# Two-layer inference step on one core: everything behind the mixing in two token halves, with the pages' attention interleaved with the mixing and the first half

## The chip, the cores and the metric

The kernel runs on one core of a Trainium2 chip. The metric is the device time of one execution in microseconds (us); less is better. A core has a matrix engine (TensorE, in the profile PE, with its weight loads as PEld), a vector engine (VectorE, DVE), a scalar engine (ScalarE, ACT), a general engine (GpSimd, POOL), and SyncE (SP), which here issues most of the transfers. Each engine works through its own list of instructions in order and waits at semaphores for the others.

## The reference

One step of a hybrid decoder with two layers, D = 1024, for a prompt of 1024 tokens and for 8 samples with 4 new tokens each, which share all weights. Per layer, each part ahead of its residual add begins with an RMS norm:

```python
z = rms_norm(x, norm_mix) @ w_in                 # one projection for all heads
o_gdn, s_new = gated_delta_rule(...)             # 4 DeltaNet heads, causal short convolution before
keys = concatenate([past_k, kd]); vals = concatenate([past_v, vd])   # samples: 4096 past tokens in pages
o_diff = diff_attention(qd, keys, vals, ...)     # 4 differential attention heads
x = x + concatenate([o_gdn, o_diff]) @ w_out
qc = rms_norm((rms_norm(x, norm_cross) @ w_cq).reshape(B, L, 4, 128), qnorm_cross)
x = x + memory_attention(qc, mem_k, mem_v).reshape(B, L, 512) @ w_co     # 256 memory tokens
hf = rms_norm(x, norm_ffn)
gt, ffn_new = causal_dwconv(hf @ w_gate, ffn_buf, conv_ffn)              # width 3 along the tokens
x = x + (silu(gt) * (hf @ w_up)) @ w_down                                # 2816 wide
```

Of the parts behind `o_diff`, only the convolution in the MLP links tokens with each other: a token needs the gate rows of the two tokens before it. The next layer's mixing needs all tokens.

## The kernel before

The residual stream is kept with features on the partitions: 8 tiles of 128 features by 1056 columns, the 1024 prompt tokens and then the 32 sample tokens. A product of two float32 operands is made of three matmuls: each operand is split into a rounded part and a rest (ScalarE casts, VectorE or GpSimd subtracts), and `mm3` (L346 to L348) adds high by high, low by high and high by low. Weights come from DRAM in units of 512 KB: a load by SyncE into one of two `raw` buffers (L322), a cast on ScalarE (L325, tile `whi`) and a subtraction on GpSimd (L326, tile `wlo`), into four buffers of each (`Weights(..., 2, 4)`).

A layer has two stages. In the **mixing**, the projections, DeltaNet (`gdn`, tiles with psG) and the prompt's attention (`attn`) are Python generators that `interleave` runs side by side by their costs; beside all of them run the pages (`dec`, then `dec_end`): page loads by SyncE (`kn`, `vn`), a transpose on VectorE (L639), scores (L643) and values (L667) on TensorE. Such an interleaving only sets the order in which instructions are handed to a scheduler; the scheduler then writes each engine's list by priorities and by a simulated time line (`prio` shifts the priority). The mixing leaves its outputs in DRAM, `ogs` and `oas`, by tiles of tokens; only the last attention head goes through SBUF (`lasts`).

**Behind the mixing**, everything runs once over all 1056 columns in three chunks of CH = 352 (`csl`): the output projection (`linear_add`, its last two feature tiles chunk by chunk, and a norm as soon as a chunk is complete), the cross-attention (projection of the queries; `cross_prompt` by token tiles of 128, interleaved with `cross_samples`), `w_co`, the next norm, and the MLP in pairs of feature tiles (FG = 2): per tile the gate and the up products, the convolution and the multiplication, and then per pair the down products, added to `x` (L1986). In `norm_chunk` ScalarE squares, VectorE adds, TensorE sums over the features with a matrix of ones, ScalarE makes the inverse root, and VectorE and GpSimd scale and split. After the last pair the first layer's chunks are normed for the next layer and written to DRAM (`xsc`); after the second layer the tiles are transposed and written out.

PSUM banks for the stream are taken in turn (`psA`, four); behind the mixing a fifth (`psB`) joins them (`turn[0] = 1`).

## Time and profile before

| | |
|---|---|
| Three runs | 4203.21, 4212.04 and 4216.07 us; median 4212.04 |
| The profiled execution | 4210.3 us from its first to its last instruction; its time outside that span isn't listed |
| Mean granted TensorE clock | 0.948 |
| TensorE, weight loads | 3816.0 us (91%), 3397.5 us (81%) |
| VectorE, ScalarE, GpSimd | 2314.2 us (55%), 1259.7 us (30%), 1150.3 us (27%) |
| DMA | 581.55 MB, 138 GB/s over the span |

Read along time, the first layer's mixing lasts until about 1104 us, its pages from 190 to 1050; its output projection starts at 1110.58, and its MLP lasts until about 2139. The second layer's mixing follows, and what is behind that ends at 4210.3. A share of the span is an average over these stages; what a stage is bound by is seen in a window of it. An engine that is idle costs nothing unless another engine waits for it, and the waits of TensorE show where that is so.

### The profile page before, as it was taken

To read this page: it belongs to the slowest core of one execution; us is meant where nothing else is said; L and a number is where in the kernel's file an instruction comes from. 1 tells how busy PE (TensorE), PEld (TensorE's weight loads), DVE (VectorE), ACT (ScalarE), POOL (GpSimd) and SP (SyncE) were. 2 spreads that over 40 slices of the span, in tenths; PEclk is the share of its full clock that TensorE was granted. 3 is DMA by queue.
4 is the path that set the end of the run, shared out by engine and by line. 5 is a ranking of instruction groups with operands and counts; after the bars stand their busy time and mean duration, and the time that the engine had idled before them with its cause. 6 is when DMAs were issued, how large, how long until landed. Compare 5 with 4: busy or idle time off the path is not lost. (4 is left out here: it accounts for less than half of the span.)

```text
span 4210.3 us, 74231 instructions
## 1 busy us (share of the span) xinstructions
PE 3816.0 (91%) x27524; PEld 3397.5 (81%) x27524; DVE 2314.2 (55%) x4305; ACT 1259.7 (30%) x2773; POOL 1150.3 (27%) x1130
## 2 busy tenths in 40 slices
PE   6988888888899999999988889877879999999999
PEld 5877765565798999999977777745669889999999
DVE  7554655666445644444477456556753564545454
ACT  4322423333334312121233134332342531212121
POOL 6641321311331322222235223122123132222221
PEclk8999998898899999999999999988989999999999
DMA  5698889998412111111139988899732211111111
GB/s 176 195 277 224 226 222 230 234 234 218 142 46 81 46 46 46 46 46 46 49 114 282 267 229 221 237 247 241 202 103 87 87 40 46 46 46 46 46 46 57
DMA packets 549602, 581.55 MB, mean 138 GB/s; under 512 B 67053, under 2 KB 376248, under 8 KB 549240
## 3 DMA queue, kind: packets, MB, share of 16 engines
q1 hardware_dynamic: 503765, 546.67, 47.4%
q10 hardware_dynamic: 43811, 25.81, 2.1%
q8 instruction: 217, 3.56, 0.4%
q0 software_dynamic: 1664, 4.33, 0.3%
q14 instruction: 145, 1.19, 0.1%
HBM read 498.45 MB, written 78.20 MB: 137 GB/s over the span
## 5 line engine op out<-in xcount | busy, mean ns | idle before, releaser
L346 PE MATMUL psA<-hh,whi 128*128 128x352 f32 x3072 | 1012.6, 330 | 27.1 <-ACT whi L325 23.0
L347 PE MATMUL psA<-hl,whi 128*128 128x352 f32 x3072 | 1004.7, 327 | 0.8 <-POOL hl L384 0.8
L348 PE MATMUL psA<-hh,wlo 128*128 128x352 f32 x3072 | 1001.8, 327 | 0.0
L326 POOL TENSOR_TENSOR wlo<-raw,whi 128x1024 fp32r<-128x1024 f32 (+1 forms) x308 | 529.6, 1727 | 1361.6 <-ACT whi L325 1353.2
L346 PEld LDWEIGHTS psA<-hh,whi 128*128 128x128 f32 x3072 | 587.2, 191 | 39.6 <-ACT whi L325 28.2
L347 PEld LDWEIGHTS psA<-hl,whi 128*128 128x128 f32 x3072 | 588.8, 192 | 10.8 <-issue 8.3
L348 PEld LDWEIGHTS psA<-hh,wlo 128*128 128x128 f32 x3072 | 585.9, 191 | 12.6 <-issue 11.2
L325 ACT CAST whi<-raw 128x1024 fp32r<-128x1024 f32 (+1 forms) x308 | 236.8, 781 | 898.6 <-issue 436.7
L639 DVE STREAM_TRANSPOSE T<-kn 128x1024 f32<-128x1024 f32 x256 | 315.9, 1237 | 197.5 <-DMA kn<-in_cache_k_dram 195.0
L346 PE MATMUL psA<-hi,hh 128*128 128x256 f32 (+3 forms) x864 | 253.2, 294 | 48.4 <-DVE cxn L730 44.6
L1986 DVE TENSOR_TENSOR x<-x,psA 128x352 f32<-128x352 f32 x422 | 214.3, 520 | 134.4 <-PE psA L348 130.4
L346 PE MATMUL psA<-ah,whi 128*128 128x352 f32 x844 | 275.4, 326 | 0.0
L347 PE MATMUL psA<-al,whi 128*128 128x352 f32 x844 | 271.2, 321 | 0.0
L348 PE MATMUL psA<-ah,wlo 128*128 128x352 f32 x844 | 266.2, 325 | 0.0
L348 PE MATMUL psA<-hi,hl 128*128 128x256 f32 (+3 forms) x864 | 249.3, 290 | 3.9 <-POOL hl L384 3.3
L347 PE MATMUL psA<-lo,hh 128*128 128x256 f32 (+3 forms) x864 | 250.2, 290 | 0.0
L667 PE MATMUL psC<-vn,pT 128*32 128x512 f32 x1024 | 148.7, 674 | 103.7 <-DMA vn<-in_cache_v_dram 86.0
L346 PEld LDWEIGHTS psA<-hi,hh 128*128 128x128 f32 (+1 forms) x864 | 160.0, 186 | 60.4 <-issue 42.2
L643 PE MATMUL psB<-T,lq 128*32 128x128 f32 x4096 | 147.3, 289 | 63.8 <-DVE T L639 41.1
L347 PE MATMUL psB<-hl,whi 128*128 128x352 f32 x576 | 188.1, 327 | 10.3 <-DVE hl L384 7.1
L346 PE MATMUL psB<-hh,whi 128*128 128x352 f32 x576 | 188.7, 328 | 6.9 <-ACT hh L381 6.9
L1956 DVE COPY fraws<-psA 128x32 f32<-128x32 f32 x36 | 6.9, 191 | 341.0 <-ACT fraw L1955 341.0
(528 smaller groups left out, 7317.1 us busy)
## 6 DMA issues: line engine op xcount, KB each, us to landing
kn<-in_cache_k_dram SPq DMA_DIRECT2D x512, 256.0 KB
vn<-in_cache_v_dram SPq DMA_DIRECT2D x512, 256.0 KB
raw<-in_w_gate_dram SPq DMA_DIRECT2D x44, 512.0 KB
raw<-in_w_up_dram SPq DMA_DIRECT2D x44, 512.0 KB
raw<-in_w_down_dram SPq DMA_DIRECT2D x44, 512.0 KB
qksc<-ctt ACTq DMA_DIRECT2D x128, 128.0 KB
raw<-in_w_in_dram SPq DMA_DIRECT2D x128, 128.0 KB
gdsc<-cdst SPq DMA_DIRECT2D x24, 528.0 KB
```

The costliest lines, as they stand in the source:

```text
L325: s_.copy(hi, raw)
L326: g_.tensor_tensor(lo, raw, hi.bitcast(F32), op=ALU.subtract)
L346: t_.matmul(ps, ahi, bhi, start=(i == 0), stop=False)
L347: t_.matmul(ps, ahi, blo, start=False, stop=False)
L348: t_.matmul(ps, alo, bhi, start=False, stop=(i == n - 1))
L639: v_.transpose(T[:, 2 * hf:2 * hf + 2].rearrange("p s j b -> p (s j b)"), kn.rearrange("p s d -> p (s d)"))
L643: t_.matmul(sc[32 * c:32 * c + 32, (S % 4) * P:(S % 4 + 1) * P], lq[:, 4 * c + j, :], T[:, :, 4 * c + j, :], start=(j == 0), stop=(j == 3))
L667: t_.matmul(po[32 * i:32 * i + 32, :], pT[:, i, S, :], vn[:, i, :], start=(S == 0), stop=(S == 7))
L1956: v_.tensor_copy(raws[:, :, 2:6], ps[:, NP - 2 * CH:CH].rearrange("p (b t) -> p b t", t=4))
L1986: v_.tensor_tensor(x[:, ot, cs], x[:, ot, cs], ps[:, 0:CH], op=ALU.add)
```

## The change

The generator `post(lo, n, smp)` does all that stood behind the mixing, for `n` prompt tokens from `lo` on and, if `smp`, for the sample tokens too. It is run with tokens 0 to 511, in two chunks of 256 (in the MLP one of 512, except for its first feature tile and its last down products), and then with tokens 512 to 1023 and the samples, in two chunks of 272. Each half loads and splits its weights. The first is chained behind the mixing in the stream that is interleaved with the pages, and the two streams' totals are changed from 527 against 128 to 950 against 152. The two last gate columns of the first half go to the second in `carry`. In the first layer the residual stream of each half goes to `xsc`; the norms for the next layer are made in the second half, those of tokens 0 to 511 from columns that are read back (`early`, at two places of its MLP), those of the rest behind its last down products. In the second layer each half writes its output. The last attention head's output goes through DRAM like the others'. `norm_chunk` takes any columns, and its sum and its root share a buffer name. The fifth PSUM bank joins in the second half only. Comments are gone, which shifts lines: L346 before is L347 after.

```diff
+POST = 500.0
...
+    def __init__(self, pool, name, n=NT):
+        self.pool, self.name, self.n = pool, name, n
+        self.t = [pool.tile([P, KT // 2, n], F32R, tag=f"{name}{i}", name=f"{name}{i}") for i in range(2)]
...
-    def norm_chunk(c, x, gain, hh, hl, wk, light=False, nb=1, late=0):
-        """RMS norm of a chunk, in two parts. light: little work for the vector engine."""
-        cs = csl(c)
-        acc = None if light else wk.tile([P, CH], F32, name="nacc", tag="nacc", bufs=nb)
+    def norm_chunk(cs, xk, gain, hh, hl, wk, light=False, nb=1, late=0):
+
+
+        w = cs.stop - cs.start
+        acc = None if light else wk.tile([P, w], F32, name="nacc", tag="nR", bufs=nb)
         ps = psG()
         for kk in range(4):
-            sq = wk.tile([P, 2, CH], F32, name="nsq", tag="nsq", bufs=2 * nb)
-            s_.activation(sq, x[:, 2 * kk:2 * kk + 2, cs], AF.Square)
+            sq = wk.tile([P, 2, w], F32, name="nsq", tag="nsq" if light else "nhf", bufs=4 if light else 3)
...
+        R = wk.tile([P, w], F32, name="nR", tag="nR", bufs=nb)
...
+    carry = cp.tile([P, FT, 2], F32, name="carry")
...
-                if h < 3:
-                    QX(13).dma_start(oas[c][:, h, :], od)
-                else:
-                    lasts.append((c, od))
+                QX(13).dma_start(oas[c][:, h, :], od)
...
-        for _ in interleave((rest(), 80 + 172 + 45 + 230.0), (chain(ahead(dec(), TUNE[6]), ahead(dec_end(), TUNE[8])), 8 * TUNE[0] * (float(XP[16]) if l == 0 else 1))):
...
+        w_cm, nw_cm, X_cm = (pool(f"{nm}{l + 1}", side=HS) for nm in ("w", "nw", "X"))
+        W = nw = X = None
...
+        def post(lo, n, smp):
+
+
+            nonlocal W, nw, X, Hn_cm, hn, ln, prep_cm, pre_next
+            NL = n + (NS if smp else 0)
+            SUB = NL // 2
+            subs = [slice(0, SUB), slice(SUB, NL)]
+            tiles = [(lo // P + i, P) for i in range(n // P)] + ([(8, NS)] if smp else [])
+            if W is None:
+                W = Weights(w_cm.__enter__(), 2, 4)
+            with prio(UPRI):
+                us = [unit(a["w_out"][l], KT, k) for k in range(int(XP[9]))]
+            if nw is None:
+                nw = nw_cm.__enter__()
+                X = X_cm.__enter__()
+            Hp_cm = pool(f"P{l}{lo}", side=HS)
+            Hp = Hp_cm.__enter__()
+            hh = Halves(Hp, "ph", NL)
+            hl = Halves(Hp, "pl", NL)
+            for i, (t, w_) in enumerate(tiles):
+                cs = slice(i * P, i * P + w_)
+                ot_ = stp.tile([P, KT * P], F32, name="ot", tag="ot", bufs=2).rearrange("p (k t) -> p k t", t=P)
+                for hf in range(2):
+                    o_ = ot_[:, 4 * hf:4 * hf + 4, 0:w_]
+                    nc.sync.dma_start(o_, ogs[t] if hf == 0 else oas[t // 4][:, :, (t % 4) * P:(t % 4) * P + w_])
+                    split(hh.t[hf][:, :, cs], hl.t[hf][:, :, cs], o_, g_ if (hf == 0 and OSP) or OSP > 1 else v_)
+            x = X.tile([P, KT, n + NS], F32, name="x", tag="x", bufs=1)
+            for k in range(KT):
+                nc.sync.dma_start(x[:, k, 0:NL], xsc[:, k, lo:lo + NL])
+            yield 1.0
...
+            wv = int(XP[9])
+            for ot, c in wave(wv, wv, 2) + [(t, c) for t in range(wv, 6) for c in range(2)] + [(t, c) for c in range(2) for t in (6, 7)]:
+                cs = subs[c]
+                ps = lin_ps(us[ot][0], us[ot][1], hh, hl, KT, cs)
+                v_.tensor_tensor(x[:, ot, cs], x[:, ot, cs], ps, op=ALU.add)
+                if c and wv - 1 <= ot < 5:
+                    us.append(unit(a["w_out"][l], KT, ot + 1))
+                if ot == 5:
+                    us.append(unit(a["w_out"][l], KT, 6 + c))
+                yield 24 * SUB / 2200.0
+                if ot == 7:
+                    norm_chunk(cs, xat(x, cs), g_cross, hh, hl, nw)
+                    yield 0.5
...
+            ssp = psG((P, 17)) if not smp else psC((P, 17))
...
+                nt = n // P
...
+            yield from interleave((cross_prompt(), n / P * 2.7 + 7), *([(cross_samples(), 8 * 2.5 + 3)] if smp else []))
...
+            if smp and more:
+
+                Hn_cm = pool(f"H{l + 1}", side=XS)
+                Hn = Hn_cm.__enter__()
+                hn, ln = Halves(Hn, "hh"), Halves(Hn, "hl")
+                xp = [ln.t[i][:, :, 0:lo].bitcast(F32) for i in range(2)]
+                for i in range(2):
+                    nc.sync.dma_start(xp[i], xsc[:, 4 * i:4 * i + 4, 0:lo])
+
+                def early(c):
+                    cs = slice(c * 256, c * 256 + 256)
+                    norm_chunk(cs, lambda k, m: xp[k // 4][:, k % 4:k % 4 + m, cs] if m > 1 else xp[k // 4][:, k % 4, cs], pv[l + 1][:, 48:56], hn, ln, nw)
...
+            for th in range(2):
+                for c in range(2):
+                    cs = subs[c]
+                    for ot in range(4 * th, 4 * th + 4):
+                        u = wco[ot // 2]
+                        oc = slice(P * (ot % 2), P * (ot % 2) + P)
+                        ps = lin_ps(u[0][:, :, oc], u[1][:, :, oc], hh, hl, 4, cs)
+                        v_.tensor_tensor(x[:, ot, cs], x[:, ot, cs], ps, op=ALU.add)
+                        yield 12 * SUB / 2200.0
+                    if th:
+                        norm_chunk(cs, xat(x, cs), g_ffn, hh, hl, nw)
+                        yield 0.5
+                    elif c:
+                        nxt = gu(0)
+
+
+            wide = subs if smp else [slice(0, NL)]
+            f0 = 0
+            while f0 < FT:
...
+                    if lo:
+                        g_.tensor_copy(raw[:, 0:2], carry[:, f])
+                    else:
+                        g_.memset(raw[:, 0:2], 0.0)
...
+                    chs = wide if f else subs
+                    order = [(kind, cs) for cs in chs for kind in "gu"] if f == 0 else [(kind, cs) for kind in "gu" for cs in chs]
...
+                        if not smp:
+                            g_.tensor_copy(carry[:, f], raw[:, n:n + 2])
+                            return None
...
+                        if more and f in (4, 8):
+                            early(f // 4 - 1)
...
+                chs = subs if lastg else wide
+                for ot, cs in [(ot, cs) for cs in chs for ot in range(8)]:
+                    w_ = cs.stop - cs.start
+                    ps = psA()[:, 0:w_]
+                    mm3(ps, [((dn[fi][0][:, ot], dn[fi][1][:, ot]), (ah[:, fi, cs], al[:, fi, cs])) for fi in range(gs_)])
+                    v_.tensor_tensor(x[:, ot, cs], x[:, ot, cs], ps, op=ALU.add)
+                    yield 3 * gs_ * w_ / 2200.0
+                    if lastg and ot == 7 and more:
+                        if smp:
+                            norm_chunk(slice(lo + cs.start, lo + cs.stop), xat(x, cs), pv[l + 1][:, 48:56], hn, ln, nw)
+                        s_.dma_start(xsc[:, :, lo + cs.start:lo + cs.stop], x[:, :, cs])
+            ff_cm.__exit__(None, None, None)
+            if not more:
+                with pool(f"xout{lo}", side=XS) as ip:
+                    for i, (t, m) in enumerate(tiles):
...
+        HALF = NP // 2
+        for _ in interleave((chain(rest(), post(0, HALF, False)), 450.0 + POST), (chain(ahead(dec(), TUNE[6]), ahead(dec_end(), TUNE[8])), 152.0)):
             pass
-        turn[0] = 1
...
+        turn[0] = 1
+        for _ in post(HALF, HALF, True):
+            pass
...
```

The order of the instructions at three places. First TensorE, where the first layer's mixing ends. L667 before and L674 after are the pages' value products, L987 and L1198 parts of DeltaNet, L1422 and `oraw` the prompt's attention, and the products with `whi` the first of the output projection. Before:

```order
L667 MATMUL psC<-vn,pT 32x512 x4
L1422 MATMUL psA<-aV,aT 128x128 x4
...
L1422 MATMUL psA<-aV,aT 128x128 x8
L1439 MATMUL psA<-c_ident,oraw 128x128 x4
L346 MATMUL psA<-hh_16392,whi 128x352
L347 MATMUL psA<-hl_16394,whi 128x352
```

After:

```order
L674 MATMUL psC<-vn,pT 32x512 x4
L987 MATMUL psG<-X,U 128x128 x4
...
L1445 MATMUL psA<-c_ident,oraw 128x128 x4
L1080 MATMUL psG<-c_ident,oy 128x128 x4
L347 MATMUL psA<-ph_13237,whi 128x256 x3
L348 MATMUL psA<-pl_13239,whi 128x256
```

The first row of each is the pages' last value product of the layer. In the whole list it is row 3455 before and row 3442 after; the first product of the output projection is row 3547 before and row 3544 after. Its width went from 352 to 256 columns.

Then SyncE at the same place: `vn` is a page's values, `raw<-in_w_out` a unit of the output projection's weights, `ot` the operands of that projection by token tiles, from DeltaNet (`og`) and attention (`oa`), and `x<-xsc` the residual stream. Before:

```order
L608 DMA vn<-in_cache_v_dram 32x4x512
...
L1692 DMA mv<-out_p_mem_v_dram 128x2x512
L263 DMA c_sel_17313<-in_cst_dram 128x32
L1673 DMA ot<-og_78 128x512
L1673 DMA ot<-oa_85 128x3x128
L1673 DMA ot<-og_79 128x512
L1673 DMA ot<-oa_85 128x3x128
L322 DMA raw<-in_w_out_dram 128x8x128 x2
L1673 DMA ot<-og_80 128x512
```

After:

```order
L615 DMA vn<-in_cache_v_dram 32x4x512
...
L1448 DMA oa_86<-od 128x512
L323 DMA raw<-in_w_out_dram 128x8x128 x2
L1083 DMA og_83<-gate 128x512
L1660 DMA x<-xsc 128x512 x3
L323 DMA raw<-in_w_out_dram 128x8x128
L1660 DMA x<-xsc 128x512 x5
L323 DMA raw<-in_w_out_dram 128x8x128
L1683 DMA mkT<-msc 128x1024
L1656 DMA ot<-og_78 128x512
L1656 DMA ot<-oa_85 128x4x128
```

The first row is again the last page load. Four of the operand loads stood ahead of the first weights; now the weights and the residual stand ahead of the first operands, and a store of the attention's output (`oa_86<-od`) ahead of the weights.

Last TensorE in the cross-attention: `mkT,qc` are scores of the prompt (256 memory tokens), `mkn` transposes of the samples' memory keys, `cred` sums for the norm of the queries, and `phx` transposes of probabilities. Before, all tokens:

```order
L1752 MATMUL psA<-mkT,qc 128x256 x4
L1823 MATMUL psG<-c_ident,mkn 128x128 x8
L396 MATMUL psC<-cred,c_sel_17313 32x8 x4
L397 MATMUL psC<-cred,c_sel_17313 32x1
L1752 MATMUL psA<-mkT,qc 128x256 x2
L1752 MATMUL psB<-mkT,qc 128x256 x2
L1752 MATMUL psA<-mkT,qc 128x256 x2
L1823 MATMUL psG<-c_ident,mkn 128x128 x8
```

After, the first half:

```order
L1716 MATMUL psG<-cred,c_sel_14182 32x4 x4
L1749 MATMUL psA<-mkT,qc 128x256 x6
L1716 MATMUL psG<-cred,c_sel_14182 32x4 x4
L1749 MATMUL psA<-mkT,qc 128x256 x2
L1716 MATMUL psG<-cred,c_sel_14182 32x4 x4
L1749 MATMUL psA<-mkT,qc 128x256 x4
L1772 MATMUL psG<-c_ident,phx 128x128 x4
L1749 MATMUL psA<-mkT,qc 128x256 x2
L1772 MATMUL psG<-c_ident,phx 128x128 x4
L1749 MATMUL psA<-mkT,qc 128x256 x2
L1772 MATMUL psG<-c_ident,phx 128x128 x8
L1782 MATMUL psA<-plx,mv 128x256 x4
```

The samples' products that stood between the prompt's are in the second half now; the first has the prompt's alone.

## Rows read from the trace of the kernel before

**Rows 1.** Windows: busy us of each engine, with counts, clock and DMA; mixing, MLP

```profile
core 0: us, PE busy (x) PEld busy (x) DVE busy (x) ACT busy (x) POOL busy (x), PEclk, DMA share, GB/s
190.00:1050.00 860.00, 727.93 (x6243) 563.39 (x6244) 502.41 (x1023) 276.75 (x725) 210.22 (x298) 0.91 0.91 235
1500.00:2100.00 600.00, 600.00 (x3735) 592.81 (x3735) 286.90 (x465) 114.13 (x170) 136.83 (x102) 1.00 0.16 47
```

**Rows 2.** Waits of TensorE on the pages: us in total, times, longest us

```profile
PE psC L667 <- DMA vn<-in_cache_v_dram: 86.0, 49, 4.3
PE psB L643 <- DVE T L639: 41.1, 36, 5.9
```

**Rows 3.** Windows: two norms, cross-attention of both layers, change of layer, end

```profile
1200.00:1240.00 40.00, 36.00 (x218) 34.41 (x217) 34.01 (x42) 18.50 (x29) 20.50 (x11) 1.00 0.09 27
1355.00:1385.00 30.00, 22.36 (x113) 20.20 (x111) 27.49 (x35) 14.81 (x21) 16.15 (x9) 0.83 0.12 35
1255.00:1330.00 75.00, 72.02 (x586) 59.46 (x585) 39.93 (x99) 41.05 (x109) 4.50 (x5) 1.00 0.33 106
3300.00:3360.00 60.00, 55.46 (x425) 43.73 (x418) 34.51 (x87) 38.16 (x104) 3.62 (x4) 0.97 0.32 97
2139.00:2178.00 39.00, 26.92 (x163) 24.77 (x161) 35.27 (x61) 17.48 (x26) 16.03 (x18) 0.87 0.29 97
4194.00:4210.30 16.30, 9.71 (x78) 8.28 (x77) 5.18 (x8) 6.54 (x12) 0.00 (x0) 0.96 0.69 266
```

**Rows 4.** Timeline of TensorE: start us, us; products of four widths

```profile
1700.01 0.32 PE L346 MATMUL psA<-hh,whi 128*128 128x352 f32 x1
...
1704.63 0.32 PE L348 MATMUL psB<-hh,wlo 128*128 128x352 f32 x1
...
258.33 0.28 PE L346 MATMUL psA<-hi,hh 128*128 128x256 f32 x1
...
259.92 0.28 PE L348 MATMUL psA<-hi,hl 128*128 128x256 f32 x1
...
2168.45 0.29 PE L347 MATMUL psA<-lo,hh 128*128 128x264 f32 x1
...
2169.92 0.28 PE L347 MATMUL psA<-lo,hh 128*128 128x264 f32 x1
...
101.83 0.39 PE L348 MATMUL psM<-whi,mlo 128*128 128x512 f32 x1
...
105.79 0.39 PE L347 MATMUL psM<-wlo,mh 128*128 128x512 f32 x1
```

**Rows 5.** Groups of ScalarE in 1255 to 1330 us: busy, mean ns, idle before

```profile
L1763 ACT ACTIVATE hhx<-psA,cmx,rq 128x256 f32<-128x256 f32 x18 | 10.0, 594 | 0.0
L1763 ACT ACTIVATION_READ_ACCUMULATOR hhx<-psA,cmx,rq 128x1 f32 x18 | 4.2, 235 | 0.0
L1776 ACT COPY hlx<-psG 128x512 f32<-128x512 f32 x9 | 5.1, 610 | 1.4 <-PE psG L1775 1.3
```

**Rows 6.** Chain that ended last, second layer's cross-attention: start us, us

```profile
3331.47 0.86 PE psB L1752 x4
3344.02 3.45 PE psA L1785 x16
3354.47 0.44 PE psG L1775 x4
```

**Rows 7.** Page: splitting of weights, whole span: busy, mean ns, idle before

```profile
L326 POOL TENSOR_TENSOR wlo<-raw,whi 128x1024 fp32r<-128x1024 f32 (+1 forms) x308 | 529.6, 1727 | 1361.6 <-ACT whi L325 1353.2
L325 ACT CAST whi<-raw 128x1024 fp32r<-128x1024 f32 (+1 forms) x308 | 236.8, 781 | 898.6 <-issue 436.7
```

**Rows 8.** Timeline of SyncE and TensorE: first output-projection load and product

```profile
1104.17 1.06 SPq L322 DMA_DIRECT2D raw<-in_w_out_dram  x2
1110.58 0.66 PE L346 MATMUL psA<-hh,whi 128*128 128x352 f32 x1 [7.69 <-ACT whi L325]
```

More of the change, by code (lines that the diff above doesn't have):

```diff
@@ L370, in norm_chunk @@
             with prio(late):
-                t_.matmul(ps[:, 0:CH], ones, acc, start=True, stop=True)
-        R = wk.tile([P, CH], F32, name="nR", tag="nR", bufs=nb)
-        s_.activation(R, ps[:, 0:CH], AF.Ln, scale=1.0 / D, bias=epsc)
+                t_.matmul(ps[:, 0:w], ones, acc, start=True, stop=True)
+        R = wk.tile([P, w], F32, name="nR", tag="nR", bufs=nb)
+        s_.activation(R, ps[:, 0:w], AF.Ln, scale=1.0 / D, bias=epsc)
         s_.activation(R, R, AF.Exp, scale=-0.5)
@@ L1329, in build @@
         at_cm = pool(f"at{l}", side=HS)
-        lasts = []
         def attn():
```

643 lines of the change are left out of this document (291 added, 352 removed).

## The prediction

> **What bounds the kernel now.** I read the windows by stage first, then the waits, then single instructions. In the long stretch behind the mixing, TensorE is busy in all of 600 us at a granted clock of 1.00 [rows 1]: there the matmul stream is the bound, with VectorE at 287 of 600 us, ScalarE at 114 and GpSimd at 137. While the pages stream beside the mixing the DMA share is 0.91 and TensorE is busy in 728 of 860 us [rows 1]. The waits name the pages there: 86.0 us for page values and 41.1 us for a transpose of page keys [rows 2]. So this kernel has two kinds of idle time that the change could touch: some 130 us of page waits in the mixing, and short joints of 3 to 12 us behind it, where a norm, the cross-attention, the next layer or the output starts [rows 3].
>
> **The change, part by part.** All below is against the profiled execution's own 4210.3 us span; the median of the runs is 1.7 us above it.
>
> *The pages.* The words of the change let the pages run beside the first half. The order of the changed kernel does not. On TensorE the last pages' product still stands about a hundred rows ahead of the first product of the output projection, as before, and on SyncE the last page load stands ahead of the first load of that projection's weights. Engines take their instructions in this order, so all pages end inside the mixing and the page waits of [rows 2] stay. I price this part at 0; below zero only if the pages moved (a rival below), above zero not, since the order in the mixing is nearly the same.
> The rows show why nothing slides over by itself: TensorE stood 86.0 us at the page products [rows 2] although other products stood behind them. The Trainium skill (TensorE: Matmul & The Clock Gate, Part 2, step ①) says the same, that matmuls stay in program order and only weight loads are pulled ahead; by it the page waits cannot move, and the sum keeps its 0.
>
> *The products.* Behind the mixing before has 11,808 products of 352 columns; the order of the changed kernel has 1,920 of 256, 2,976 of 512 and 7,872 of 272 (both 4,156,416 columns). Start to start, from [rows 4]: 352 columns (1704.63 − 1700.01)/29 = 0.1593 us; 256 columns (259.92 − 258.33)/14 = 0.1136; 264 columns (2169.92 − 2168.45)/12 = 0.1225; 512 columns (105.79 − 101.83)/17 = 0.2329. No row has 272: scaled from 256 it is 0.1207, from 264 it is 0.1262, from 352 it is 0.1231. Before: 11,808 × 0.1593 = 1881.0 us. After: 1,920 × 0.1136 + 2,976 × 0.2329 + 7,872 × 0.1231 = 218.1 + 693.1 + 969.0 = 1880.2, so −1; with the two other prices −20 and +24. I take 352's price per column because that stretch, with weight loads for every product, is the same work.
> The Trainium skill (same page, Back-to-back issue gap) gives an isolated gap of N/2.4 + 2.5 ns, a fixed price for each product that speaks against splitting. By it before is 11,808 × 149.2 ns = 1761.4 us and after 1763.8, an estimate of +2. The trace has 159.3 ns where the formula has 149.2, so its level does not hold here, and the sum goes by the rows.
>
> *The norms.* The cross-attention's norm left TensorE 4.0 us idle in its 40 us window, the feed-forward norm 7.6 in 30 us, at a clock of 0.83; VectorE was busy in 34 of 40 and 27.5 of 30 us [rows 3], so it paces them. A chunk of 352 takes it about a third of that 34 us, 11.3 us, covered by the last two tiles of the last chunk, 2 × 24 × 0.1593 = 7.6 us: 3.7 us stays bare, near the 4.0 seen. A half-width chunk takes about 8.3 us (11.3 × 264/352) against a cover of 2 × 24 × 0.1136 = 5.5: 2.8 bare. Now the norm's sum and its root share one buffer, so the second chunk's cannot overlap the first's; I take 4.5. There are twice as many: 2 × 4.5 − 4.0 = +5 for the first kind and 2 × 7.3 − 7.6 = +7 for the second, and +3 for the lowered clock once more: +15 a layer. Ends: 0 (bare time scales with width) to 25 (nothing covers the 8.3).
>
> *Cross-attention.* Before, the samples' products and the prompt's eight tiles fill each other's gaps: 3.0 us idle of 75, 4.5 of 60 [rows 3]. The first half has four tiles and no samples. ScalarE per tile: 4 × (0.594 + 0.235) for the exponentials and their sums and 2 × 0.610 for copies [rows 5], 4.5 us; four tiles 18. TensorE per tile: four scores in 0.86 and eight transposes at four in 0.44, 0.88; the 16 value products of all four tiles 3.45 [rows 6]: 4 × 1.74 + 3.45 = 10.4. Idle 18 + 4.5, one tile's chain as lead and tail, − 10.4 = 12, and 3 for the clock behind it: +15. The second half keeps the samples, and the idle time of before with them. Ends: 0 (copies go to VectorE) to 25.
>
> *MLP of the first half.* One chunk of 512. Between the last up product of a pair and the down products that need it stand 9 products, 9 × 0.2329 = 2.1 us, for a multiplication, a cast and a subtraction of 512 columns, each near the 0.610 of a 512-column copy [rows 5] or somewhat over: 1.8 to 2.7. Eleven pairs × up to 0.6: I take +3; ends 0 to 27.
>
> *Weights twice.* Gate, up, down and the three projections are loaded and split again: 164 more units, × 1727 ns on GpSimd = 283 us and × 781 ns on ScalarE = 128 us [rows 7]. Cover: the products, with GpSimd at 137 and ScalarE at 114 of 600 us [rows 1]. Price 0; without cover see the first rival.
>
> *Joints.* Between the halves the second half's operands are split while the last down products run (96 × 0.1136 = 10.9 us): +2 a layer (0 to 15). Between the mixing and the first half SyncE now issues two more weight units and the residual ahead of the first operands, and a unit waits for a raw buffer (cast and subtraction, 0.8 + 1.7 us [rows 7]). Before, the first product came 6.4 us behind the first weight load [rows 8]; now the operands come about 11 behind it, and the load itself waits for the last attention output: +9 in the first layer, +3 in the second, where they stand ahead: +12 (0 to 25). At the change of layer 12.1 us were idle [rows 3]; the norms of tokens 0–511 are now made early, in the second half's MLP, and only the last two chunks are late, behind 117 ready products: −12 (−16 to 0). The tail had 6.6 us idle [rows 3], and half of the output leaves earlier: −2.
>
> Sum: −1 + 2 × (15 + 15 + 3 + 2) + 12 − 12 − 2 = +67. Span 4277, median 4279 us.
>
> **The rivals.**
> *Slower still:* the first half is paced by its weights. A unit now lasts 24 × 0.2329 = 5.6 us instead of 72 × 0.1593 = 11.5. From load to first use took 6.4 us [rows 8], over two raw buffers some 3.5 a unit, plus GpSimd's 1.7: it should hold, but if a unit takes 6.6 it is 1 us × 66 units × 2 = +130 on the forecast, about 4400.
> *The pages move after all:* if the chip ran the pages' loads slower than the order supposes and the products behind filled in, the waits of [rows 2], 127 us, would go: 4279 − 127 = 4150. Against it: the order of both engines.
> *Not slower:* the joints scale with their width. Two half-width joints then cost what one did: norms 0 instead of +30, cross-attention 0 instead of +30 since copies move to VectorE and the clock stays up, and products at the low price, −20, with −16 at the change of layer. It decides once the joints of a layer add less than 18 us together: 4195 to 4212. For it: the bare 2.8 us above is below the 4.0 of before. Against it: the first half has no samples to fill with, and a clock of 0.83 behind a norm [rows 3].
> That the pages do not do what the words say is part of the forecast itself.
>
> **How the numbers follow.** Forecast 0.74, slower still 0.06, pages move 0.03, not slower 0.17. Of the last 0.06 ends below 4199, 0.11 within 0.3% (12.6 us, about what can be told from no change); 0.02 of the forecast lies within it too. Faster 0.03 + 0.06 = 0.09, same 0.13, slower 0.78. Range: the forecast with the ends of its terms half used gives 4225 to 4340; with part of the fourth case 4207 to 4342.
>
> **What would show it.** In the trace after: page products that end ahead of the first output-projection product, and waits for pages of about 127 us as before (the first step); pitches of 0.114, 0.123 and 0.233 us for the three widths; 4 to 5 us idle at each of four cross norms and about 7 at each feed-forward norm; about 12 us idle in each first half's cross-attention with ScalarE busy; under 3 us idle at the change of layer. It would be wrong if page products stood beside the first half, if TensorE were idle between units in its MLP, or if the total came out under 4225.

## The result and the profile after

The changed kernel took 4403.16 us (4398.64 to 4409.45, four runs) against 4209.64 for the kernel before: 1.0457 times as long, 95% interval 1.0441 to 1.0474. The profiled execution spans 4399.9 us, 189.6 more than before. 67 were forecast; the sign was right, the size was not.

The phases of both executions in us, first layer / second layer, read off the timeline by these marks: the first output-projection load (in the second half, the last down product of the first), the first score, the last value product of the cross-attention, the first and the last down product:

| phase | before | after, both halves | more |
|---|---|---|---|
| output projection, norm, queries | 155.8 / 157.2 | 183.8 / 182.8 | 28 / 26 |
| cross-attention | 63.4 / 67.0 | 75.2 / 75.0 | 12 / 8 |
| its output, norm, first MLP tiles | 101.2 / 101.3 | 114.0 / 115.5 | 13 / 14 |
| MLP from the first to the last down product | 724.6 / 722.7 | 790.2 / 775.2 | 66 / 53 |
| mixing and change of layer | | | −7 / −17 |
| end | 15.3 | 10.3 | −5 |

The MLP holds 118 of the 190 us. In windows of the kernel after (columns as in [rows 1]) the first layer's first half has its MLP in the first row, the second half in the second:

```profile
1282.00:1649.00 367.00, 352.48 (x1540) 282.45 (x1539) 192.39 (x202) 102.11 (x131) 163.85 (x105) 0.99 0.32 96
1837.00:2261.00 424.00, 401.07 (x3032) 390.55 (x3031) 260.56 (x481) 125.65 (x194) 176.25 (x130) 0.97 0.27 81
1222.00:1282.00 60.00, 51.48 (x340) 47.76 (x339) 35.56 (x56) 22.90 (x35) 24.20 (x17) 0.89 0.20 62
1783.00:1837.00 54.00, 45.28 (x344) 43.38 (x334) 37.30 (x62) 23.79 (x38) 26.68 (x20) 0.94 0.30 98
```

Where [rows 1] shows TensorE busy in all of 600 us, it now stands 15 and 23 us idle, and GpSimd is busy in 42 to 45% of the time instead of 23%. The last two rows hold the feed-forward norms of the two halves: 8.5 and 8.7 us idle, where the one norm of before had 7.6 [rows 3].

What TensorE waited for (us in total, times, longest us), first the pages:

```profile
PE psC L674 <- DMA vn<-in_cache_v_dram: 84.3, 48, 6.2
PE psB L650 <- DVE T L646: 47.5, 34, 4.3
...
PE psA L347 <- ACT ph L383: 35.3, 11, 4.9
...
PE psA L348 <- DVE al L309: 18.5, 23, 2.4
...
PE psA L347 <- DVE fcv L1999: 12.2, 19, 3.3
...
PE psA L349 <- POOL wlo L327: 10.5, 16, 1.4
```

The two page waits are those of [rows 2] (86.0 and 41.1). `ph` is the norms' rounded part; its name before is `hh`, with 13.3 us. New are the MLP's: `al`, the rest of the down products' operand, which VectorE subtracts, and `fcv`, the multiplication that frees an accumulator. One such wait in full, GpSimd, VectorE and TensorE in the kernel after (start us, us, and in brackets the idle time before):

```profile
1321.26 2.40 POOL L327 TENSOR_TENSOR wlo<-raw,whi 128x1024 fp32r<-128x1024 f32 x1 [1.46 <-ACT whi L326]
1320.27 0.69 DVE L1999 TENSOR_TENSOR fcv<-fcv,psA 128x512 f32<-128x512 f32 x1 [0.70 <-ACT fcv L295]
1321.73 2.48 DVE L309 TENSOR_TENSOR al<-fcv,ah 128x512 fp32r<-128x512 f32 x1 [0.77 <-ACT ah L308]
1322.95 0.64 PE L347 MATMUL psA<-ah,whi 128*128 128x512 f32 x2
1324.26 0.95 PE L348 MATMUL psA<-al,whi 128*128 128x512 f32 x3 [0.68 <-DVE al L309]
```

GpSimd subtracts a unit of weights until 1323.66. VectorE's `al` begins 0.47 us behind the start of that, ends 0.55 us behind its end, and takes 2.48 us. The multiplication of the same width, which was done before GpSimd began, took 0.69. TensorE waits for `al`.

### The profile page after: what moved, and what is told of

Read it like the earlier page. It is cut to its first block, busy times and chain, and to the rows that moved or that the text cites. A ratio compares the mean times of both kernels' runs of the same rounds, so it can differ in the third digit from the quotient of the medians.

```text
span 4399.9 us, 78002 instructions
## 1 busy us (share of the span) xinstructions
PE 3886.3 (88%) x28558; PEld 3324.8 (76%) x28558; DVE 2513.4 (57%) x4572; ACT 1466.1 (33%) x3071; POOL 1571.0 (36%) x1402
## 5 line engine op out<-in xcount | busy, mean ns | idle before, releaser
L327 POOL TENSOR_TENSOR wlo<-raw,whi 128x1024 fp32r<-128x1024 f32 (+1 forms) x472 | 932.4, 1983 | 1135.5 <-ACT whi L326 1105.3
L347 PE MATMUL psA<-ph,whi 128*128 128x272 f32 (+2 forms) x2784 | 880.5, 319 | 64.2 <-ACT ph L383 35.3
L348 PE MATMUL psA<-pl,whi 128*128 128x272 f32 (+2 forms) x2784 | 879.3, 317 | 14.0 <-POOL pl L386 14.0
L349 PE MATMUL psA<-ph,wlo 128*128 128x272 f32 (+2 forms) x2784 | 877.9, 316 | 0.0
L347 PEld LDWEIGHTS psA<-ph,whi 128*128 128x128 f32 x2784 | 533.4, 193 | 100.5 <-ACT ph L383 37.6
L348 PEld LDWEIGHTS psA<-pl,whi 128*128 128x128 f32 x2784 | 535.3, 192 | 47.8 <-POOL pl L386 17.0
L349 PEld LDWEIGHTS psA<-ph,wlo 128*128 128x128 f32 x2784 | 534.1, 192 | 28.7 <-POOL wlo L327 0.2
L347 PE MATMUL psA<-ah,whi 128*128 128x272 f32 (+2 forms) x948 | 304.4, 336 | 20.1 <-DVE fcv L1999 12.2
L348 PE MATMUL psA<-al,whi 128*128 128x272 f32 (+2 forms) x948 | 304.2, 333 | 18.5 <-DVE al L309 18.5
L349 PE MATMUL psA<-ah,wlo 128*128 128x272 f32 (+2 forms) x948 | 289.5, 331 | 10.5 <-POOL wlo L327 10.5
L347 PE MATMUL psA<-hi,hh 128*128 128x256 f32 (+3 forms) x864 | 254.7, 296 | 41.4 <-DVE cxn L737 33.7
L347 PE MATMUL psA<-hh,whi 128*128 128x352 f32 x768 | 257.7, 336 | 0.0
L348 PE MATMUL psA<-hl,whi 128*128 128x352 f32 x768 | 257.5, 335 | 0.0
L349 PE MATMUL psA<-hh,wlo 128*128 128x352 f32 x768 | 255.2, 333 | 0.0
L674 PE MATMUL psC<-vn,pT 128*32 128x512 f32 x1024 | 144.5, 655 | 110.0 <-DMA vn<-in_cache_v_dram 84.3
L650 PE MATMUL psB<-T,lq 128*32 128x128 f32 x4096 | 152.2, 295 | 86.8 <-DVE T L646 47.5
```

The source lines that it names most:

```text
L327: g_.tensor_tensor(lo, raw, hi.bitcast(F32), op=ALU.subtract)
L347: t_.matmul(ps, ahi, bhi, start=(i == 0), stop=False)
L348: t_.matmul(ps, ahi, blo, start=False, stop=False)
L349: t_.matmul(ps, alo, bhi, start=False, stop=(i == n - 1))
L650: t_.matmul(sc[32 * c:32 * c + 32, (S % 4) * P:(S % 4 + 1) * P], lq[:, 4 * c + j, :], T[:, :, 4 * c + j, :], start=(j == 0), stop=(j == 3))
L674: t_.matmul(po[32 * i:32 * i + 32, :], pT[:, i, S, :], vn[:, i, :], start=(S == 0), stop=(S == 7))
```

## The experiments

Times are medians beside runs of the kernel before on the same chip (4211 to 4214 us). "Changed" is the kernel after.

**Do the pages move? `apart`.** The pages are interleaved with the mixing alone:

```diff
-        for _ in interleave((chain(rest(), post(0, HALF, False)), 450.0 + POST), (chain(ahead(dec(), TUNE[6]), ahead(dec_end(), TUNE[8])), 152.0)):
+        for _ in interleave((rest(), 80 + 172 + 45 + 230.0), (chain(ahead(dec(), TUNE[6]), ahead(dec_end(), TUNE[8])), 8 * TUNE[0] * (float(XP[16]) if l == 0 else 1))):
             pass
+        for _ in post(0, HALF, False):
+            pass
```

> The interleaving taken back: the pages run beside the mixing alone, with the totals of before (527 against 128 or 8 x 16), and the first half follows by itself. Theory (the time went into more joints behind the mixing, TensorE idle there and the lower clock that follows; the interleaving with the pages changed nothing, since the pages' instructions stood ahead of the first half anyway): 4403 us, within 13. Rival (the new interleaving itself costs, by a worse order in the mixing): 30 us or more below 4403, with the page waits of TensorE (132 us) smaller.

4403.6 us, as expected. The new interleaving changed nothing that can be measured.

**And if they do? `held`.** A page load that is written behind the start of the first half is queued behind the first half's residual loads (`issue_after`):

```diff
+                if hold:
+                    st_.enter_context(tc.issue_after(hold.pop().ins))
```

> The page loads that are written behind the start of the first half (about the last half of each layer's pages) are queued on SyncE behind the first half's residual loads, so that they do run beside it, as the words of the change say. Theory (the words did not come true, and the joints of the first half are idle time that pages can fill): the mixing of each layer shortens by the page waits of its last part, the pages' products fill joints; 60 to 140 us below 4403, that is 4263 to 4343, and the idle time of TensorE falls by as much. Rival 1 (TensorE takes its instructions in order, so pages in the first half only put their waits there): 4403 within 20. Rival 2 (page loads and weight loads collide in the first half): above 4423.

4376.9 us (1.0387, 1.0366 to 1.0408): 26 below changed, outside all three expectations. In windows of mixing and first half, the changed kernel's two rows first, then those of `held`:

```profile
190.00:1097.00 907.00, 765.59 (x6539) 599.48 (x6538) 541.59 (x1126) 300.31 (x798) 221.43 (x304) 0.91 0.88 225
1097.00:1617.00 520.00, 473.57 (x2434) 397.57 (x2435) 261.57 (x333) 167.23 (x254) 227.68 (x144) 0.96 0.31 95
```

```profile
190.00:960.00 770.00, 681.16 (x5432) 553.98 (x5433) 472.06 (x1012) 286.18 (x771) 214.78 (x301) 0.92 0.68 187
960.00:1617.00 657.00, 560.88 (x3543) 439.93 (x3542) 340.97 (x440) 188.10 (x289) 230.35 (x148) 0.93 0.65 165
```

The mixing is 137 us shorter and the first half 137 longer; in sum TensorE is as busy as before. The wait for page values went on (103.9 us in all). The second layer, by the same marks, gained 13 us. Pages beside other work gained little here: they take TensorE's time wherever they stand, and TensorE, which works in order, waited for them there too.

**The early norms, `early_last`.** The calls of `early` stand behind the last down products.

> The norms of tokens 0 to 511 for the next layer are made behind the last down products of the second half, not at two places of its MLP. In the first layer the second half's MLP had 10 us more idle time and 19 us more in all than in the second layer. Theory (the early norms cost about 19 us there and save about as much at the change of layer, since VectorE has to do them somewhere): 4403 within 13, the MLP of the first layer's second half at 405 us instead of 423, the change of layer longer by 15 to 25 us. Rival (they are a loss, their VectorE time could be hidden behind the next layer's first products): 15 to 25 us below 4403.

4404.8 us; the second half's MLP in the first layer took 407.5 us instead of 423.4, and the change of layer took as much more. As expected: the early norms move time and save none.

**One chunk or two, `no_wide`.** `wide = subs` in the first half too.

> The first half's MLP in two chunks of 256 columns instead of one of 512. Products cost the same by their pitch (5,952 x 0.1169 = 696 us against 2,976 x 0.2337 = 695). Theory (the down products wait at each of 22 pairs for one chain of multiplication, cast and subtraction of 512 columns, 9 us a layer): with chunks the chain of the last chunk is half as long, the waits on it halve: 5 to 15 us below 4403 in all. Rival (the wait moves: four accumulators do not suffice for two gate and two up chunks, and the up products wait for the multiplication that frees them): 4403 or up to 40 us above.

4446.1 us (1.0545, 1.0519 to 1.0572): 43 above changed, just over the rival's 40. Its waits:

```profile
PE psA L347 <- DVE fcv L1999: 34.0, 60, 3.3
...
PE psA L349 <- POOL wlo L327: 28.2, 34, 1.4
```

Both grew (12.2 and 10.5 in the changed kernel): narrower chunks uncover VectorE's and GpSimd's work.

**The halving alone, `one_piece` and `one_piece2`.** The generator runs once over 1,056 columns, behind the pages; `one_piece2` also has the interleaving total of the kernel before in the cross-attention, the edit in the middle.

```diff
-            SUB = NL // 2
+            nch = 3
+            SUB = NL // nch
...
-            yield from interleave((cross_prompt(), n / P * 2.7 + 7), *([(cross_samples(), 8 * 2.5 + 3)] if smp else []))
+            yield from interleave((cross_prompt(), n / P * 2.7 + 14), *([(cross_samples(), 8 * 2.5 + 3)] if smp else []))
...
-        for _ in post(HALF, HALF, True):
+        for _ in post(0, NP, True):
             pass
```

> The changed kernel with the halving alone taken back: the generator runs once over all 1,056 columns in three chunks of 352 behind the pages, with the fifth accumulator; the last attention head through DRAM, the weights' priorities and the norm's shared buffer stay as changed; the columns carried over and the early norms are gone with the halves. Theory (what was lost is the halving: twice the joints, with their idle time and the lower clock behind each, and waits in the narrower MLP): 4200 to 4225. Rival (the other edits cost a good part): above 4240.

> The undivided version again, with the cross-attention's interleaving total for the prompt as in the kernel before (8 x 2.7 + 14, not + 7). Theory (of its 56 us over before, 14.5 were waits for the samples' memory values, which that total brought on; the rest lies at the end of the mixing and in the norms): 4248 to 4260. Rival (the waits for these values have another reason): 4268 within 8.

4268.5 and 4226.8 us (1.0029, 1.0012 to 1.0047). The first looked like a loss by the other edits; the second shows that 42 of its 56 us came with that total, more than was expected. So the other edits cost 14 us, and the halving 176 (4403 less 4227). (The halved kernel has the changed total too; TensorE's waits for the samples' memory values, which went with it, are 14.5 us in `one_piece` and 4.2 in the changed kernel.)

**Gate products ahead of the down products, `pipe`.** The next pair's first gate products are emitted ahead of a pair's down products:

```diff
+                if not lastg:
+                    f = f0
+                    (ghi, glo), (uhi, ulo) = nxt
...
+                    order = [("g", cs) for cs in wide]
...
+                    gated = True
                 chs = subs if lastg else wide
```

> The changed kernel, but in the MLP the gate products of the next pair's first feature tile stand ahead of the down products of the pair before, so that the multiplication, cast and subtraction have 5.6 to 6 us of cover. Theory (the waits for al, ah and fcv in front of the down products, 18.5 + 5.8 + 17 us, are a cover that got too short): 4403 less 15 to 45, and those waits nearly gone. Rival (the accumulators are what is short: gate and up chunks and the down products share four or five banks): 4403 within 13 or above, and the waits for fcv grow.

4333.8 us (1.0299, 1.0267 to 1.0331): 69 below changed, more than the theory's 45. The wait for `al` fell from 18.5 to:

```profile
PE psA L348 <- DVE al L309: 5.6, 4, 2.4
```

With the edit of `held` as well (`pipe_held`) it was 4318.2 us (1.0244, 1.0222 to 1.0265), inside the 4295 to 4322 that were expected if the two add; 4325 or more was the rival. They nearly add: 85 us below changed, where 69 and 26 make 95.

**Keeping TensorE busy in the joints, `warm`.**

```diff
+            with tc.issue_after(last.ins):
+                for _ in range(n):
+                    t_.matmul(ps[:, 0:P], ident, ident, start=True, stop=True)
```

> The changed kernel with the pages beside the mixing alone (4403.6 us), and in each of the eight joints of a norm (cross and feed-forward, both halves, both layers) 32 matmuls of the identity with itself, 128 columns each, put on TensorE behind the last product ahead of the joint; nobody reads them. They take about 32 x 0.112 = 3.6 us of the 4 to 9 us that TensorE stands idle there. Theory (each joint is followed by 6.8 us or more at half clock, which costs as much again as half of it; a TensorE kept busy in the joint keeps its clock): the stretches of half clock at those joints vanish, 10 to 14 fewer of them, 25 to 50 us below 4403. Rival (the clock falls for another reason, or the dummy products only delay): 4403 within 13, or up to 20 above.

4400.1 us: the rival's time. The feed-forward norms of the first layer's halves in `warm`, to set beside the last two rows of the first windows above:

```profile
1228.00:1287.00 59.00, 55.70 (x403) 51.98 (x402) 35.72 (x57) 22.49 (x35) 24.59 (x18) 0.97 0.21 63
1791.00:1845.00 54.00, 51.02 (x396) 49.28 (x396) 37.45 (x61) 24.06 (x38) 26.85 (x21) 1.00 0.31 98
```

The granted clock rose from 0.89 and 0.94 to 0.97 and 1.00, TensorE was busy where it had stood, and the stretches are as long as they were. So TensorE's clock does not set their length. VectorE is busy for 36 to 37 us in each, with the norm that TensorE waits for; that it paces them is a reading of the rows, and no run tests it.

**Weights twice in the kernel before, `twice` and `twice_vec`.** Each unit behind the mixing is loaded and split twice; in the second version, whose edit this is, VectorE subtracts.

```diff
-            s_.copy(hi, raw)
-            g_.tensor_tensor(lo, raw, hi.bitcast(F32), op=ALU.subtract)
+            for _ in range(self.times):
+                raw = self.p.tile([P] + sh, F32, tag="raw", bufs=self.nraw, name="raw")
+                nc.sync.dma_start(raw, src)
+                s_.copy(hi, raw)
+                self.eng.tensor_tensor(lo, raw, hi.bitcast(F32), op=ALU.subtract)
...
+        W.times = 2
+        W.eng = v_
```

> The kernel before, with every weight unit behind the mixing loaded and split twice (the second pass writes the same values again), so GpSimd, ScalarE and the weight loads have the doubled work of the changed kernel in the undivided MLP. Theory (that work is hidden beside the products): 4205 to 4225. Rival (the doubled splitting is itself a good part of the 190 us, because the split of a unit comes late): 4240 or more, with TensorE waiting for wlo.

> The kernel before with each weight unit behind the mixing loaded and split twice, the subtractions on VectorE (on GpSimd: 4356 us). Theory (the 143 us were mostly a chain of two loads, casts and subtractions into the same tiles, which comes late, and the queue of loads behind it): 4290 to 4345. Rival (they were mostly VectorE held up by GpSimd): below 4260.

4355.9 us (1.0349, 1.0320 to 1.0379) and 4236.8 (1.0066, 1.0045 to 1.0087). The theory fell both times, and the times are the rivals', though in `twice` TensorE waited more for casts (`whi`, 79.7 us; 23.0 before) than for `wlo` (12.9). 119 of the 143 us go when GpSimd does not do it; here two passes follow each other in one tile (two subtractions of 2.4 us, or two of 1.2), so this pair does not part a late unit from a held-up VectorE.

**Without the subtractions, `nosplit`, and with nobody waiting for them, `ghost`.** Both leave out the rest of each weight behind the mixing, so they give other results and serve for their times alone. `nosplit`:

```diff
+            if self.whole:
+                s_.copy(hi, raw)
+                return hi, hi
```

`ghost`, in which the subtraction still runs:

```diff
-            return hi, lo
+            return (hi, hi) if self.whole else (hi, lo)
```

> The changed kernel without the second part of the weights behind the mixing: the unit's subtraction on GpSimd and its tile are left out, and the products that took it take the rounded part again, so TensorE's list is the same and the loads and casts too. Left out is the rest of each of those weights. Theory (in the changed kernel the doubled splitting is nearly hidden: TensorE waits 10.5 us for wlo in all, and a unit comes 1.7 us earlier where it is waited for): 4373 to 4393. Rival (the doubled splitting is a large part of the 190 us, as doubling it in the kernel before cost 143 us): below 4353.

> The changed kernel with the weights' subtraction on GpSimd as it is, but the products that took its result take the rounded part again (left out is the rest of each weight): nothing on TensorE waits for the subtraction, while GpSimd is as busy and holds the raw buffers as long. Theory (a: GpSimd's subtractions hold VectorE's instructions up): 4385 to 4405, no gain beyond the 10.5 us of waits for wlo. Rival (b: the units come late): near the 4286 of the run without subtractions, below 4330.

4286.4 us (1.0173, 1.0155 to 1.0191) and 4364.8 (1.0377, 1.0348 to 1.0406). `nosplit` gives 117 us back: the rival. `ghost` lies between its expectations and nearer to the first: 38 us go when nothing waits for the units' second part and its tile, the other 78 come only when GpSimd stops subtracting. Some of TensorE's waits in `ghost`, then in `nosplit`; `pl` is the rest that GpSimd subtracts in the norms:

```profile
PE psA L350 <- POOL pl L388: 24.3, 10, 2.9
PE psA L350 <- DVE al L309: 14.3, 22, 2.4
PE psA L349 <- ACT whi L328: 9.0, 2, 5.5
```

```profile
PE psA L353 <- POOL pl L391: 10.6, 10, 1.2
PE psA L352 <- ACT whi L331: 1.6, 1, 1.6
PE psA L353 <- DVE al L309: 1.4, 2, 0.7
```

So the 78 us are not VectorE's `al` alone: GpSimd's own part of the norms and casts that come later are in them too.

**The subtraction on VectorE, `vec`, `pipe_vec`, `before_vec` and `before_vec2`.**

```diff
-            g_.tensor_tensor(lo, raw, hi.bitcast(F32), op=ALU.subtract)
+            self.eng.tensor_tensor(lo, raw, hi.bitcast(F32), op=ALU.subtract)
...
+                W.eng = v_
```

> The changed kernel with the weights' subtraction behind the mixing on VectorE, not GpSimd. It adds 328 instructions of about 1.2 us (twice the 0.69 us of a free one of 512 columns, less its start) = 390 us to VectorE's 2513 in all, and takes 328 x 2.45 = 800 us off GpSimd. Theory (a): al and the first step of the convolution take 0.44 to 0.70 us each, the waits for al go, 4300 to 4360. Rival (VectorE, which paces the norms, now has more to do and the units wait for it): 4390 or more.

> The changed kernel with gate products ahead of the down products (4334 us alone) and the weights' subtraction on VectorE. Theory (a: the first edit covers the held-up chain, the second takes the hold-up away, so they overlap in the MLP and add only in the norms and at the start): 4280 to 4330. Rival (they act on different things and add in full): below 4270.

> The same move in the kernel before: the weights' subtraction behind the mixing on VectorE. There the MLP had no wait on either, and al of 352 columns took 521 ns alone and 2,412 ns beside a subtraction, which the products covered. Theory (a): the MLP stays, only the norms and the start may gain or lose; 4205 to 4222. Rival (VectorE becomes the bound in the norms): 4230 or more.

> The kernel before with the weights' subtraction behind the mixing on VectorE, again, over five rounds. Theory (a start of each layer's output projection that is 2 to 7 us shorter, and shorter norms): 0.995 to 0.999 of before. Rival (chance): 1.000 within 0.002.

4313.0 us (1.0238, 1.0205 to 1.0271), 4301.8 (1.0217, 1.0189 to 1.0246), and for the kernel before 4199.4 (0.9980, 0.9964 to 0.9995; below both expectations) and again, over five rounds, 4194.8 (0.9958, 0.9940 to 0.9977; the theory). `vec` gives back 90 of the 190; it takes the hold-up away, but its units come earlier too. With `pipe` the two overlap, as the theory had it. The same edit makes the kernel before a little faster: it beats both kernels. By the marks of the table the MLP of both layers took 1447 us before, 1565 in the changed kernel, 1526 in `ghost`, 1491 in `vec` and 1478 in `nosplit`: 87 of its 118 us more go with the subtractions.

All instructions that write `al` (count, then ns min/median/max, first and last start, forms), before, after, `ghost`, `vec` and `before_vec2`:

```profile
L308 DVE TENSOR_TENSOR al<-fcv,ah x132: 501/525/2444, 1411.8 to 4173.5; 128x352 fp32r<-128x352 f32 x132
```

```profile
L309 DVE TENSOR_TENSOR al<-fcv,ah x134: 417/2394/2491, 1280.2 to 4378.4; 128x272 fp32r<-128x272 f32 x88, 128x512 fp32r<-128x512 f32 x42, 128x256 fp32r<-128x256 f32 x4
```

```profile
L309 DVE TENSOR_TENSOR al<-fcv,ah x134: 426/2412/2530, 1267.8 to 4341.6; 128x272 fp32r<-128x272 f32 x88, 128x512 fp32r<-128x512 f32 x42, 128x256 fp32r<-128x256 f32 x4
```

```profile
L309 DVE TENSOR_TENSOR al<-fcv,ah x134: 416/434/694, 1275.9 to 4294.6; 128x272 fp32r<-128x272 f32 x88, 128x512 fp32r<-128x512 f32 x42, 128x256 fp32r<-128x256 f32 x4
```

```profile
L308 DVE TENSOR_TENSOR al<-fcv,ah x132: 511/519/527, 1400.7 to 4148.7; 128x352 fp32r<-128x352 f32 x132
```

The median went from 525 to 2394 ns, with widths of mostly 272 and 512 instead of 352, and back to 434 once GpSimd no longer subtracted; in `ghost`, where TensorE does not wait for the subtraction, it stays at 2412. The largest value in the kernel before was 2444 already: there 41 of 132 met a subtraction. In the changed kernel all 42 of 512 columns did, and 40 of the 88 of 272 (mean 2312 ns; the other 48 took 441). VectorE itself needs half of GpSimd's time for a unit of weights; the subtraction's rows of after (with 128 small ones of 256 columns) and of `vec`:

```profile
L327 POOL TENSOR_TENSOR wlo<-raw,whi x472: 718/2390/2979, 75.5 to 4366.4; 128x1024 fp32r<-128x1024 f32 x116, 128x256 fp32r<-128x256 f32 x42
```

```profile
L329 DVE TENSOR_TENSOR wlo<-raw,whi x328: 1182/1224/1537, 1105.3 to 4282.1; 128x1024 fp32r<-128x1024 f32 x164
```

Other instructions of VectorE in the changed kernel: additions with one operand in PSUM, the convolution's first step (one operand in SBUF, one factor per partition) and its later steps (two operands in SBUF):

```profile
L1669 DVE TENSOR_TENSOR x<-x,psA x58: 406/422/440, 1118.6 to 3842.2; 128x256 f32<-128x256 f32 x32, 128x272 f32<-128x272 f32 x26
L1913 DVE TENSOR_TENSOR x<-x,psA x58: 411/422/439, 1223.6 to 3948.1; 128x256 f32<-128x256 f32 x32, 128x272 f32<-128x272 f32 x26
L1954 DVE TENSOR_SCALAR fcv<-fraw,pvf x88: 472/488/2522, 1272.4 to 4371.9; 128x512 f32<-128x512 f32 x88
L1958 DVE SCALAR_TENSOR_TENSOR fcv<-fraw,pvf,fcv x176: 737/750/2960, 1274.9 to 4373.3; 128x512 f32<-128x512 f32 x176
```

Of the 116 additions 46 began while GpSimd subtracted weights, and none of them took longer than 440 ns. In `ghost` the first steps moved out of the subtractions' way:

```profile
L1957 DVE TENSOR_SCALAR fcv<-fraw,pvf x88: 471/479/495, 1262.1 to 4335.1; 128x512 f32<-128x512 f32 x88
```

So its 38 us hold some hold-up beside the units' lateness, and the division into 38 and 78 is rough.

**The norm's shared buffers in the kernel before, `shared`.**

```diff
-        acc = None if light else wk.tile([P, CH], F32, name="nacc", tag="nacc", bufs=nb)
+        acc = None if light else wk.tile([P, CH], F32, name="nacc", tag="nR", bufs=nb)
...
-            sq = wk.tile([P, 2, CH], F32, name="nsq", tag="nsq", bufs=2 * nb)
+            sq = wk.tile([P, 2, CH], F32, name="nsq", tag="nsq" if light else "nhf", bufs=4 if light else 3)
...
```

> The kernel before with the norm's buffers of the changed kernel: the sum shares one buffer with the root, and the squares share three buffers with the scaled columns. Theory (this keeps the norm of one chunk from overlapping that of the chunk before; it is the part of the 56 us of the undivided version that lies in the norms): 4213 plus 5 to 25. Rival (VectorE paces the norms anyway): 4213 within 8.

4207.7 us (0.9991, 0.9976 to 1.0006): no cost, the rival.

## Why the prediction was wrong

The step that failed is "Weights twice ... Price 0". It asked whether the engines that split had time left, and they had. It did not ask what GpSimd's subtractions do to VectorE. A VectorE subtraction with both operands in SBUF stands still beside one (2.4 us instead of 0.44), and twice as many of them met VectorE chains in front of half as many products. `nosplit` puts all that the subtractions cost at 117 of the 190 us: 38 that go in `ghost`, where the units' own lateness lies, and 78 that go only without the subtractions, where VectorE's hold-up lies. How much of each these two causes are is not shown more finely. (`nosplit` also drops the subtractions that the kernel before had. Moving those to VectorE gave that kernel 12 and 19 us, so an estimate of what the doubling itself costs is 100.) All of it stood at 0. The rest of the 190 lies outside this step, in parts below.

The price of the work was misread too. The 1727 ns of [rows 7] are a mean over two forms; a unit of weights is the larger one:

```profile
L326 POOL TENSOR_TENSOR wlo<-raw,whi 128x1024 fp32r<-128x1024 f32 x180 | 435.8, 2427 | 1159.5 <-ACT whi L325 1159.2
```

So 164 units more are 398 us on GpSimd, not 283. And the sum in the rival "Slower still" comes to 3.5 + 2.4 = 5.9 us a unit, over the 5.6 that a unit lasts, where 3.5 + 1.7 seemed to hold.

The Trainium skill (SBUF — State Buffer, Who interferes with whom) says that GpSimd and VectorE share one port pair under an exclusive lock, which a VectorE instruction with two SBUF inputs needs against a GpSimd instruction that reads SBUF, and that the loser is fully blocked. The trace agrees: 441 ns alone, 2312 beside a subtraction, and no more than 440 for the additions to `x` that read PSUM and began beside one. It is the rule that spoke against this change, and its mark stood in the trace of before, in the spread of `al` from 501 to 2444 ns.

*MLP of the first half, +3 a layer.* The term was the right wait at the wrong size. With before's MLP shared out by columns, the first half took 15 and 20 us more than its share in the two layers; TensorE's waits for `ah` and `al` in it are 11.8 and 11.5 us. The chain was priced by a copy of 512 columns [rows 5]; its subtraction takes 2.4 us, not 0.6, so multiplication, cast and subtraction are 3.9 us in the wait shown (1320.27 to 1324.21) against the 2.1 of cover. The second half's MLP, which the sum left out, took 50 and 32 us more than its share; 16 of the 50 are the early norms (`early_last`), and its largest waits are `fcv` and `wlo`. `pipe`, which gives the chain more cover, got 69 us back.

*The pages, 0.* Right: waits of 84.3 and 47.5 us as before, all ahead of the first half; `apart` shows the same time. The rival in which they move was wrong in its price too: when `held` moved them, 26 us went, not 127.

*Products, −1.* About +17, inside the bounds: the average pitches are 0.1602 us for 352 columns before and 0.1169, 0.2337 and 0.1256 for 256, 512 and 272 after (0.1231 taken for the last).

*Norms, +12 idle, and cross-attention, +12 idle a layer.* In the first layer the four norms stand 28 us idle where the two of before stood 11: +17. The cross-attention stands 5.9 and 4.4 against 3.0: +7, less than forecast, since TensorE had more to do: in the first half it has 32 score and 32 value products, busy for 9.7 and 7.6 us, where the sum had 16 of each in 3.4 and 3.45. The phases that hold them grew by 28, 13 and 12 us, more than the idle time; no run takes the rest apart. *The clock, +6 a layer:* the lowered clock was there (0.89 and 0.94 in the feed-forward norms), but `warm` raised it and the time stayed, so no price of it is shown. (In the working of the norms 11.3 × 264/352 is 8.5, not 8.3; the 4.5 that was taken hardly depends on it.)

*Joints.* Of the +12 at the start of the output projection about 9 came: TensorE stood 14.1 and 10.4 us idle in the first 42 and 44 us of it, where it had stood 7.5 and 8.2 in 36 and 38. The +2 between the halves was 0 in the first layer and 1 in the second.

*Change of layer −12 and end −2.* The end is −5. The −12 was no gain: the table's −17 holds some mixing, and what the change of layer saves, the early norms take in the second half's MLP; `early_last` puts them back and the time is the same.

*The rivals.* "Slower still" named 4400 us, and the time is that, by another way: units that come late are at most some 38 us of it, not 130. "Not slower" asked for joints that scale with their width; the feed-forward norm of a half stood 9 us idle like that of the whole.

Some 100 us remain between `pipe_vec` and `before_vec`, in which the subtractions do not run beside VectorE: in the first layer 21 in the output projection with its norm, 12 in the cross-attention, about 15 around the second norm and 14 in the MLP, by the same marks as in the table (a tile of gate products, 11.6 us, counted back to the MLP). No run takes these apart further.

## What to carry to other kernels

When a change doubles the work of an engine with time to spare, ask which other engine its instructions hold up, and look at the spread (least, median, largest) of the instructions beside it, not at the mean: two levels in one group of the same width were a collision here. When a stage is cut in two, every chain that one set of products covered is to be covered by half as many; price that chain from its own rows, collisions included. And read in the order of the built program whether the instructions that are meant to move do.

## What the runs showed of the hardware

- Not only `al` was held up. Of the convolution's 88 first steps of 512 columns in the changed kernel 41 took 1.9 to 2.5 us, the others 482 ns on average; of its 176 later steps 14 took 2.6 to 3.0 us, the others 747 ns. An average over each group would have hidden that. The additions to `x` with an operand in PSUM were not held up (at most 440 ns).
- A granted clock of 0.89 and 0.94 in two norms cost nothing that `warm` could win back: at 0.97 and 1.00 the stretches were as long.
- The same subtraction of 128 x 1024 takes a median of 1.22 us on VectorE and 2.4 on GpSimd.
